# The order of TensorE's products in a two-layer decoder trunk: kinds in larger batches, wide passes grouped by width, low parts last in the head

## The chip, the cores and the metric

The kernel runs on one core of one Trainium2 chip. Its metric is the device time of one execution in microseconds: 427.88 us is the median of three runs before the change (427.61 to 428.37). The profile shows one further execution.

## What is computed

The reference is a trunk of two layers for 256 tokens of width 1024, in float32. Layer 0 makes one input projection of its normalised tokens, and its columns feed three groups of heads: a sparse attention with a compressed, a selected and a window branch (8 heads), a causal block attention (8 heads), and attention to 256 memory tokens (4 heads). Each group is gated, and one output projection adds the result to the tokens. Layer 1 does the same with retention (4 heads of width 256 and values of width 512) and a second memory attention. Cut to its frame:

```python
h = rms_norm(x, norm_g)
(nq, nkc, ..., ng, nz, mq, mk, mv, mz, eq, ez) = _split(h @ w_in, EVEN_SPLITS)
a_out = nsa_attention(rot(nq), kc, vc, rot(nks), heads(nvs), rot(nkw), heads(nvw), gates)
b_out = moba_attention(rot(mq), rot(mk), heads(mv))
m_out = memory_attention(heads(eq), mem_n, w_mem_kv)
x = x + concat([a_out * silu(nz), b_out * silu(mz), m_out * silu(ez)]) @ w_out   # layer 0
...
r_out = head_group_norm(retention(q, k, v))
x = x + concat([r_out * silu(rz), m_out * silu(ez)]) @ w_out                     # layer 1
return rms_norm(x, final_norm_g)
```

## The kernel before

Nearly all of the work is projections, and each of them is done with operands split in two: a high part that is rounded to the type fp32r, and a low part that is the rest. `split` makes the two parts of a loaded block of weights (`raw`): ScalarE writes the high part (`whi`) and VectorE the low part (`wlo`), so the low part is always the later one. A product of full precision is then three products in fp32r: high by high, high by low, and low by high (`mm3`).

TensorE runs four kinds of product here, which the planner numbers: 0 is fp32r on the full array, 1 is float32 on the full array (the 128x128 transposes above all), 2 is float32 with 64 rows of the array (the scores of a pair of heads), and 3 is float32 with 64 columns (the weights by the values). A float32 product that is no transpose runs as two passes and stands as two records in the profile.

The projections come in three shapes. `project` and its sisters have 512 columns of weights as the moving operand, and two banks of PSUM (one for each half of the tokens). `turned_unit` and `first_columns` have the weights as the stationary operand and 256 tokens as the moving one. `project_wide` has the weights as the stationary operand too and moves both parts of the tokens at once (512 columns) past the high part of the weights, and then the high part of the tokens (256 columns) past the low part; its four rounds of 128 rows (`j`) and its two banks (`ct`) make a unit, and two units (`u`) make a pass.

The order of the instructions is not that of the code. Every operation is recorded by `Plan` first, with its dependences, and `arrange` lists them greedily: twelve rounds of `once`, each followed by `dues`, and the round with the earliest end is kept. In `once` each engine takes the next operation by `order`. TensorE's rule has these parts: an operation that became ready less than 250 ns ago (`SLACK`) comes last; in a stretch of kinds 2 and 3 these come first; in kind 0 an operation of another kind goes ahead only if it has been ready for `HOLD` ns; otherwise the order of recording decides. `turn` is the planner's price for a change of kind. The other engines and the DMA queue on SyncE go by `op.due`, the time by which `dues` says that a result is wanted, worked out backwards from the times (`op.goal`) that TensorE's operations had in the round before. What `fixed()` surrounds (the head: the first two projections, up to `first_rows` of the last unit) is kept in the order of the code.

Names in the rows below and in the profile: `bpj` (3 banks), `bs` (2), `btr`, `bt` and `bo` (1 each) are the eight banks of PSUM; `big` holds the split tokens (`xh`, `xl`), `y` and `ym` the split outputs of the heads; `p` and `pt` are the weights of a softmax and their transposes; `vcr` and `yf` are the compressed values and a gated output before its split. All engine instructions are issued from one line, so that they are told apart by these names.

The prediction speaks of the head (`first_rows`, `turned_unit`), of the wide passes (`project_wide`), and of `sparse_pair`, which fills the one bank `bo` and has it emptied by a multiply of `gated` on VectorE (`yf<-bo,v`) before the next pair may begin to fill it.

Of the kernel before, what the change touches and what calls it, by code (L numbers as in the profile page):

```python
# [16 lines left out]
P = 128  # L17
T = 256
# [36 lines left out]
SLACK = 250  # L55
HOLD = 1000
FETCH = 6000
LEAD = 0


class Plan:
# [158 lines left out]
    def turn(self, mode, kind):  # L220
        if mode == kind:
            return 0
        return 95 * (mode > 1 or kind > 1) + (105 if mode > 1 else 6) * (kind == 0)

# [23 lines left out]
    def dues(self, done):  # L248
        at = None
        for op in done:  # L250
            if op.lane == "PE":
                op.goal = op.t if at is None or op.t < 16000 else max(at, 16000)
                at = op.goal + op.spent
        for op in reversed(done):
            due = op.goal if op.lane == "PE" else 1e9
            for other, full in op.next:
                if not full:
                    due = min(due, other.due - other.cost)
                elif other.lane == "PE":
                    due = min(due, other.goal - self.LAG["PE"] - LEAD * (other.kind > 0))  # L260
                else:
                    due = min(due, other.due - other.cost - self.LAG[other.lane] - (FETCH if other.lane == "SP" else self.TAIL[other.lane]))
            op.due = due

    def once(self):
# [8 lines left out]
        while len(done) < len(ops):  # L274
# [30 lines left out]
            for other, full in op.next:  # L305
                other.held -= 1
                if full:
                    other.at = max(other.at, t if other.lane == l == "PE" else op.end + self.LAG[other.lane])
                if not other.held:
                    ready[other.lane].append(other)  # L310
# [22 lines left out]
def trunk(  # L333
# [125 lines left out]
    def turned_unit(ps, lhs, wh, wl, kts, cts):  # L459

        hi, lo = lhs
        for ct in cts:
            for j, kt in enumerate(kts):
                c = slice(j * 512 + ct * P, j * 512 + ct * P + P)
                mm3(ps[ct // 2][:, (ct % 2) * T : (ct % 2 + 1) * T], wh[:, c], wl[:, c], hi[:, kt], lo[:, kt],
                    kt == 0 and ct % 2 == 0, kt == KT - 1, True)

    def project_turned(src, idx, lhs):

        ps = [bank("pj") for _ in range(2)]  # L470
        for kt, wh, wl in units(src, idx, 512):
            turned_unit(ps, lhs, wh, wl, (kt, kt + 1), range(4))
        return ps

# [13 lines left out]
    def project_wide(src, parts, both):  # L488

        for idx, half in parts:  # L490
            ps = [bank("pj") for _ in range(2)]
            for u in range(2):
                raw = load(tl("raw", [P, 1024], NRAW),
                           src[idx + u].rearrange("p (k c) -> p k c", k=4)[:, :, half * 256 : half * 256 + 256])
                wh, wl = split(raw, 1024)
                for ct in range(2):
                    for j in range(4):
                        kt = 4 * u + j
                        c = slice(j * 256 + ct * P, j * 256 + ct * P + P)
                        PE.matmul(ps[ct], wh[:, c], both[:, kt].rearrange("p h t -> p (h t)"), start=kt == 0, stop=False, skip_group_check=True)  # L500
                        PE.matmul(ps[ct][:, T:], wl[:, c], both[:, kt, 0], start=False, stop=kt == KT - 1,
                                  skip_group_check=True)
            e = tl("rot_a", [P, 512], 2).rearrange("p (k t) -> p k t", k=2)
# [100 lines left out]
    def first_rows(wh, wl, kts):  # L604

        for j, kt in enumerate(kts):
            for tok in range(2):
                ts = slice(tok * P, (tok + 1) * P)
                cs = slice(j * 512, (j + 1) * 512)
                mm3(ps_k[tok], xh[:, kt, ts], xl[:, kt, ts], wh[:, cs], wl[:, cs], kt == 0, kt == KT - 1)  # L610

# [737 lines left out]
```

## Time and profile before

| what | value |
|---|---|
| median of the runs shown | 427.88 us |
| time of the profiled execution | 428.38 us |
| span of its trace | 426.6 us |
| last product of TensorE issued | about 420 us into the span |
| TensorE busy | 418.1 us, 2312 records |
| VectorE busy | 325.7 us |
| ScalarE busy | 253.5 us |
| bytes moved | 74.21 MB |

The profiled execution lies 1.8 us over its span and 0.5 us over the median. Its records give a start and a length for each instruction. A length on TensorE includes the time in the pipeline, so lengths of neighbours overlap, and what a product costs is read from the distance between starts. Rows that merge several instructions give the first start; the distance to the next row's start, divided by their count, is the pace.

### The profile page before, as it was taken

The page shows a single profiled execution, that of the slowest core. Times are in us where ns is not written, and L with a number is a line of the kernel's source. Part 1 is how long each engine was busy: PE and PEld are TensorE (multiplying, and loading weights), DVE is VectorE, ACT ScalarE, POOL GpSimd, SP SyncE. Part 2 cuts the span into 40 slices and gives each one's busy share as a digit, 9 for nine tenths or more (in the row PEclk, how much of TensorE's full clock was granted, in tenths as well). Part 3 has the DMA queues.
Part 4 walks back from the last instruction along what each step waited for, and adds up shares of the span by engine and source line. Part 5 has one row for each costly group of instructions (what it writes and reads, how often), then busy time and mean ns, then how long its engine had stood idle before and what let it go on. Part 6 is the DMA issues. An engine that isn't in the chain of part 4 may idle for free.

```text
span 426.6 us, 6506 instructions
## 1 busy us (share of the span) xinstructions
PE 418.1 (98%) x2312; PEld 343.9 (81%) x2312; DVE 325.7 (76%) x744; ACT 253.5 (59%) x477; POOL 3.8 (1%) x11
## 2 busy tenths in 40 slices
PE   8999999999999999999999999999999999999994
PEld 7888988777777787778888888888888888888883
DVE  3789998999897476856978887786997578684624
ACT  4856638997886447945556743754553456653503
POOL 0000000000000000000000000000000000000001
PEclk9999999999999999999999999999999999999999
DMA  7988754331755844452485544365366546457302
GB/s 229 398 297 279 242 195 135 115 101 32 265 192 150 298 127 131 140 164 92 151 251 181 159 141 164 118 205 189 103 219 200 166 141 213 132 169 244 130 2 98
DMA packets 36976, 74.21 MB, mean 174 GB/s; under 512 B 3024, under 2 KB 22736, under 8 KB 36944
## 3 DMA queue, kind: packets, MB, share of 16 engines
q1 hardware_dynamic: 36512, 73.27, 52.2%
q10 hardware_dynamic: 432, 0.52, 0.3%
q8 instruction: 18, 0.29, 0.3%
q14 instruction: 14, 0.11, 0.1%
HBM read 72.74 MB, written 1.05 MB: 173 GB/s over the span
## 4 chain that ended last, share of the span: by engine, by line
PE 92%; DVE 3%; DMA 2%; ACT 1%; issue 0%; DVEq 0%; ACTq 0%
PE bpj L329 70%; PE bs L329 9%; PE btr L329 5%; PE bt L329 4%; PE bo L329 4%; DMA v<-in_xT 2%; DVE wlo L329 1%; DVE tmp L329 1%; DVE v L329 1%; DMA raw<-in_w 1%; ACT whi L329 0%; DVE p L329 0%; ACT big L329 0%; DVE rot_a L329 0%; ACT rot_a L329 0%
## 5 line engine op out<-in xcount | busy, mean ns | idle before, releaser
L329 DVE TENSOR_TENSOR wlo<-raw,whi 128x1024 fp32r<-128x1024 f32 (+3 forms) x127 | 147.0, 1165 | 56.9 <-ACT whi L329 54.4
L329 ACT CAST whi<-raw 128x1024 fp32r<-128x1024 f32 (+3 forms) x127 | 127.3, 1004 | 90.7 <-PE bpj L329 49.4
L329 PE MATMUL bpj<-whi,big 128*128 128x512 f32 (+1 forms) x496 | 150.0, 389 | 0.0
L329 PEld LDWEIGHTS bpj<-whi,big 128*128 128x128 f32 x496 | 91.3, 188 | 18.5 <-issue 1.3
L329 PE MATMUL bpj<-big,whi 128*128 128x512 f32 (+1 forms) x320 | 96.7, 382 | 0.0
L329 PE MATMUL bpj<-wlo,big 128*128 128x512 f32 (+1 forms) x248 | 87.0, 390 | 0.0
L329 PE MATMUL bpj<-big,wlo 128*128 128x256 f32 x288 | 62.7, 284 | 0.2 <-DVE wlo L329 0.2
L329 PEld LDWEIGHTS bpj<-big,wlo 128*128 128x128 f32 x288 | 52.5, 189 | 9.6 <-DVE wlo L329 0.6
L329 PEld LDWEIGHTS bpj<-big,whi 128*128 128x128 f32 x320 | 52.1, 191 | 4.2 <-issue 1.4
L329 PEld LDWEIGHTS bpj<-wlo,big 128*128 128x128 f32 x248 | 46.3, 188 | 9.4 <-issue 1.1
L329 PE MATMUL bpj<-whi,y 128*128 128x512 f32 x84 | 29.2, 396 | 0.0
L329 ACT ACTIVATE p<-p,mx 128x128 f32<-128x128 f32 (+1 forms) x48 | 21.5, 450 | 1.9 <-DVE mx L329 1.9
L329 ACT COPY pt<-bt 128x384 f32<-128x384 f32 (+1 forms) x32 | 16.1, 504 | 10.8 <-PE bt L329 9.4
L329 PEld LDWEIGHTS bpj<-whi,y 128*128 128x128 f32 x84 | 15.8, 188 | 3.1
L329 PE MATMUL bt<-cst,p 128*128 128x128 f32 x104 | 17.2, 278 | 0.0
L329 ACT ACTIVATE v<-bpj,rstd 128x512 f32<-128x512 f32 (+1 forms) x18 | 12.3, 684 | 7.9 <-PE bpj L329 7.9
L329 PE MATMUL bpj<-wlo,y 128*128 128x512 f32 x42 | 16.5, 393 | 0.0
L329 DVE CUSTOM_DVE_ANT_0 p<-bs,cst 128x128 f32<-128x128 f32 (+1 forms) x48 | 14.5, 353 | 2.4 <-PE bs L329 2.4
L329 PEld LDWEIGHTS bt<-cst,p 128*128 128x128 f32 x104 | 12.2, 140 | 4.8 <-issue 1.3
L329 DVE TENSOR_SCALAR p<-p,sm 128x256 f32<-128x256 f32 (+1 forms) x48 | 14.2, 323 | 1.0
L329 DVE TENSOR_TENSOR rot_a<-bpj,rot_a 128x256 f32<-128x256 f32 x32 | 13.3, 419 | 2.0 <-ACT rot_a L329 1.7
L329 ACT COPY rot_a<-bpj 128x256 f32<-128x256 f32 x32 | 11.7, 369 | 3.6 <-PE bpj L329 3.5
(229 smaller groups left out, 503.0 us busy)
## 6 DMA issues: line engine op xcount, KB each, us to landing
raw<-in_w SPq DMA_DIRECT2D x84, 512.0 KB, 4.2
raw<-in_wout SPq DMA_DIRECT2D x28, 512.0 KB, 3.9
raw<-in_w SPq DMA_DIRECT2D x15, 256.0 KB, 6.2
v<-in_xtok SPq DMA_DIRECT2D x4, 512.0 KB, 6.5
raw<-in_w SPq DMA_DIRECT2D x4, 280.0 KB, 3.7
v<-in_w SPq DMA_DIRECT2D x2, 512.0 KB, 4.9
raw<-in_memT SPq DMA_DIRECT2D x2, 512.0 KB, 3.6
raw<-in_memtok SPq DMA_DIRECT2D x2, 512.0 KB, 3.6
```

The lines of the kernel that those rows point to most:

```text
L329: getattr(self.engines[op.lane], method)(*args, **kw)
```

## The change

The change has three parts, and computes the same sums.

The planner. `HOLD` goes from 1000 to 2000; the prices in `turn` go up (from 105 to 150 and from 6 to 50); an operation of another kind has its goal moved back by what slack it has, up to 3000 ns (`RELAX`); and a product that depends on an earlier product counts as ready at once (0.0) and not from the time at which that one was issued. With the last, the products of one bank follow each other as they were recorded, where they took turns with another bank before.

The wide passes. All products with the high part come before those with the low part: over both banks in the first unit, and bank by bank in the second.

The head. `first_rows` and `turned_unit` go over the high weights first, with both parts of the tokens, and use the low weights last. `project_turned`, which nothing calls, is gone.

```diff
--- before.py
+++ after.py
@@ -53,9 +53,10 @@
 ROUNDS = 12
 SLACK = 250
-HOLD = 1000
+HOLD = 2000
 FETCH = 6000
 LEAD = 0
+RELAX = 3000
 
 class Plan:
@@ -220,7 +221,7 @@
     def turn(self, mode, kind):
         if mode == kind:
             return 0
-        return 95 * (mode > 1 or kind > 1) + (105 if mode > 1 else 6) * (kind == 0)
+        return 95 * (mode > 1 or kind > 1) + (150 if mode > 1 else 50) * (kind == 0)
     def arrange(self):
         ops = self.ops
@@ -252,7 +253,7 @@
                 op.goal = op.t if at is None or op.t < 16000 else max(at, 16000)
                 at = op.goal + op.spent
         for op in reversed(done):
-            due = op.goal if op.lane == "PE" else 1e9
+            due = 1e9
             for other, full in op.next:
                 if not full:
                     due = min(due, other.due - other.cost)
@@ -260,6 +261,9 @@
                     due = min(due, other.goal - self.LAG["PE"] - LEAD * (other.kind > 0))
                 else:
                     due = min(due, other.due - other.cost - self.LAG[other.lane] - (FETCH if other.lane == "SP" else self.TAIL[other.lane]))
+            if op.lane == "PE":
+                spare = due - op.spent - self.TAIL["PE"] - op.goal
+                op.goal += min(max(spare, 0), RELAX) if op.kind else 0
             op.due = due
     def once(self):
@@ -305,7 +309,7 @@
             for other, full in op.next:
                 other.held -= 1
                 if full:
-                    other.at = max(other.at, t if other.lane == l == "PE" else op.end + self.LAG[other.lane])
+                    other.at = max(other.at, 0.0 if other.lane == l == "PE" else op.end + self.LAG[other.lane])
                 if not other.held:
                     ready[other.lane].append(other)
         return free["PE"], done
@@ -459,18 +463,11 @@
     def turned_unit(ps, lhs, wh, wl, kts, cts):
         hi, lo = lhs
-        for ct in cts:
-            for j, kt in enumerate(kts):
-                c = slice(j * 512 + ct * P, j * 512 + ct * P + P)
-                mm3(ps[ct // 2][:, (ct % 2) * T : (ct % 2 + 1) * T], wh[:, c], wl[:, c], hi[:, kt], lo[:, kt],
-                    kt == 0 and ct % 2 == 0, kt == KT - 1, True)
-
-    def project_turned(src, idx, lhs):
-
-        ps = [bank("pj") for _ in range(2)]
-        for kt, wh, wl in units(src, idx, 512):
-            turned_unit(ps, lhs, wh, wl, (kt, kt + 1), range(4))
-        return ps
+        for w, x in ((wh, hi), (wh, lo), (wl, hi)):
+            for ct in cts:
+                for j, kt in enumerate(kts):
+                    PE.matmul(ps[ct // 2][:, (ct % 2) * T : (ct % 2 + 1) * T], w[:, j * 512 + ct * P : j * 512 + ct * P + P],
+                              x[:, kt], start=False, stop=kt == KT - 1 and w is wl, skip_group_check=True)
     def project_rows(src, idx, lhs, cols=512):
@@ -493,13 +490,14 @@
                 raw = load(tl("raw", [P, 1024], NRAW),
                            src[idx + u].rearrange("p (k c) -> p k c", k=4)[:, :, half * 256 : half * 256 + 256])
                 wh, wl = split(raw, 1024)
-                for ct in range(2):
-                    for j in range(4):
-                        kt = 4 * u + j
-                        c = slice(j * 256 + ct * P, j * 256 + ct * P + P)
-                        PE.matmul(ps[ct], wh[:, c], both[:, kt].rearrange("p h t -> p (h t)"), start=kt == 0, stop=False, skip_group_check=True)
-                        PE.matmul(ps[ct][:, T:], wl[:, c], both[:, kt, 0], start=False, stop=kt == KT - 1,
-                                  skip_group_check=True)
+                for cts in ((0, 1),) if u == 0 else ((0,), (1,)):
+                    for w in (wh, wl):
+                        for ct in cts:
+                            for j in range(4):
+                                kt = 4 * u + j
+                                out, x = (ps[ct], both[:, kt].rearrange("p h t -> p (h t)")) if w is wh else (ps[ct][:, T:], both[:, kt, 0])
+                                PE.matmul(out, w[:, j * 256 + ct * P : j * 256 + ct * P + P], x, start=kt == 0 and w is wh,
+                                          stop=kt == KT - 1 and w is wl, skip_group_check=True)
             e = tl("rot_a", [P, 512], 2).rearrange("p (k t) -> p k t", k=2)
             for ct in range(2):
                 S.copy(e[:, ct], ps[ct][:, T:])
@@ -603,11 +601,11 @@
     def first_rows(wh, wl, kts):
-        for j, kt in enumerate(kts):
-            for tok in range(2):
-                ts = slice(tok * P, (tok + 1) * P)
-                cs = slice(j * 512, (j + 1) * 512)
-                mm3(ps_k[tok], xh[:, kt, ts], xl[:, kt, ts], wh[:, cs], wl[:, cs], kt == 0, kt == KT - 1)
+        for x, w in ((xh, wh), (xl, wh), (xh, wl)):
+            for j, kt in enumerate(kts):
+                for tok in range(2):
+                    PE.matmul(ps_k[tok], x[:, kt, tok * P : (tok + 1) * P], w[:, j * 512 : (j + 1) * 512],
+                              start=kt == 0 and x is xh and w is wh, stop=kt == KT - 1 and w is wl)
     with plan.fixed():
         for kt in range(2):
```

The order of TensorE's instructions at three places follows. In these rows the engine is TensorE, each row is a product or several alike, out<-in.

The head, at the first projection's third round of rows (`bs_66` and `bs_67` are the two banks of `first_rows`, `bpj_64` and `bpj_65` those of `turned_unit`). Before:

```order
L329 MATMUL bs_66_126<-whi_25_85,big_12_72 128x512
L329 MATMUL bs_66_126<-wlo_29_89,big_12_72 128x512
L329 MATMUL bs_66_126<-whi_25_85,big_12_72 128x512
L329 MATMUL bs_67_127<-whi_25_85,big_12_72 128x512
L329 MATMUL bs_67_127<-wlo_29_89,big_12_72 128x512
L329 MATMUL bs_67_127<-whi_25_85,big_12_72 128x512
L329 MATMUL bpj_64_124<-big_12_72,whi_26_86 128x256 x2
L329 MATMUL bpj_64_124<-big_12_72,wlo_30_90 128x256
L329 MATMUL bpj_64_124<-big_12_72,whi_26_86 128x256 x2
L329 MATMUL bpj_64_124<-big_12_72,wlo_30_90 128x256
L329 MATMUL bpj_65_125<-big_12_72,whi_26_86 128x256 x2
L329 MATMUL bpj_65_125<-big_12_72,wlo_30_90 128x256
```

And now:

```order
L333 MATMUL bs_66_126<-whi_25_85,big_12_72 128x512
L333 MATMUL bs_67_127<-whi_25_85,big_12_72 128x512
L333 MATMUL bs_66_126<-whi_25_85,big_12_72 128x512
L333 MATMUL bs_67_127<-whi_25_85,big_12_72 128x512
L333 MATMUL bs_66_126<-wlo_29_89,big_12_72 128x512
L333 MATMUL bs_67_127<-wlo_29_89,big_12_72 128x512
L333 MATMUL bpj_64_124<-big_12_72,whi_26_86 128x256 x2
L333 MATMUL bpj_65_125<-big_12_72,whi_26_86 128x256 x2
L333 MATMUL bpj_64_124<-big_12_72,whi_26_86 128x256 x2
L333 MATMUL bpj_65_125<-big_12_72,whi_26_86 128x256 x2
L333 MATMUL bpj_64_124<-big_12_72,wlo_30_90 128x256 x2
L333 MATMUL bpj_65_125<-big_12_72,wlo_30_90 128x256 x2
```

In each group of six products the two with `wlo` stood second and fifth and now stand last; in the group of twelve narrow ones they follow each high pair before and now come after all eight.

The wide passes, around the two small products of the compression (`bs_66<-w_0_54,yf_48`): the second unit of one pass (`whi_25`, `wlo_29`) ends and the first unit of the next (`whi_26`, `wlo_30`) begins. Before:

```order
L329 MATMUL bpj_64_124<-big_12_72,whi_25_85 128x512
L329 MATMUL bpj_79_139<-big_12_72,whi_25_85 128x512
L329 MATMUL bs_66_126<-w_0_54_114,yf_48_108 128x64
L329 MATMUL bpj_79_139<-big_12_72,wlo_29_89 128x256
L329 MATMUL bpj_64_124<-big_12_72,wlo_29_89 128x256
L329 MATMUL bpj_65_125<-big_12_72,whi_26_86 128x512
L329 MATMUL bpj_64_124<-big_12_72,whi_25_85 128x512
L329 MATMUL bs_66_126<-w_0_54_114,yf_48_108 128x64
L329 MATMUL bpj_64_124<-big_12_72,wlo_29_89 128x256
L329 MATMUL bpj_64_124<-big_12_72,whi_25_85 128x512
L329 MATMUL bpj_65_125<-big_12_72,wlo_30_90 128x256
L329 MATMUL bpj_64_124<-big_12_72,wlo_29_89 128x256
```

And now:

```order
L333 MATMUL bpj_64_124<-big_12_72,wlo_29_89 128x256 x4
L333 MATMUL bpj_65_125<-big_12_72,whi_26_86 128x512 x4
L333 MATMUL bpj_79_139<-big_12_72,whi_26_86 128x512 x4
L333 MATMUL bpj_65_125<-big_12_72,wlo_30_90 128x256 x4
L333 MATMUL bpj_79_139<-big_12_72,wlo_30_90 128x256 x2
L333 MATMUL bs_66_126<-hid_84_144,w_0_54_114 64x30
L333 MATMUL bs_66_126<-w_0_54_114,yf_48_108 128x64 x2
L333 MATMUL bpj_79_139<-big_12_72,wlo_30_90 128x256 x2
L333 MATMUL bpj_65_125<-big_12_72,whi_27_87 128x512 x4
```

Before, products of 512 and of 256 columns and three banks alternate; now four products of one bank follow each other, and the low parts of the first unit come after the high parts of both banks.

The pairs of heads of the sparse attention, from the values of the first pair (`bo_81<-pt`) on; `rot_a` and `p` are transposed here. Before:

```order
L329 MATMUL bo_81_141<-pt_18_78,s_1_34_94 64x256 x2
L329 MATMUL bo_81_141<-pt_18_78,s_1_34_94 64x128 x2
L329 MATMUL bo_81_141<-pt_17_77,s_1_34_94 64x256 x2
L329 MATMUL bo_81_141<-pt_17_77,s_1_34_94 64x128 x2
L329 MATMUL btr_73_133<-cst_59_119,rot_a_44_104 128x128 x4
L329 MATMUL bpj_65_125<-big_13_73,whi_26_86 128x512
L329 MATMUL bpj_79_139<-big_13_73,whi_26_86 128x512
L329 MATMUL bo_81_141<-s_4_88_148,vcr_0_55_115 128x256
L329 MATMUL bpj_65_125<-big_13_73,wlo_30_90 128x256
L329 MATMUL bpj_79_139<-big_13_73,wlo_30_90 128x256
L329 MATMUL bo_81_141<-s_4_88_148,vcr_0_56_116 128x256
L329 MATMUL bpj_65_125<-big_13_73,whi_26_86 128x512
```

And now:

```order
L333 MATMUL bo_81_141<-pt_18_78,s_1_34_94 64x256 x2
L333 MATMUL bo_81_141<-pt_18_78,s_1_34_94 64x128 x2
L333 MATMUL bo_81_141<-pt_17_77,s_1_34_94 64x256 x2
L333 MATMUL bo_81_141<-pt_17_77,s_1_34_94 64x128 x2
L333 MATMUL bs_66_126<-s_0_33_93,v_5_9_69 128x128
L333 MATMUL bs_67_127<-s_0_33_93,v_5_9_69 128x128
L333 MATMUL bs_66_126<-s_0_33_93,v_5_9_69 128x256
L333 MATMUL bs_67_127<-s_0_33_93,v_5_9_69 128x256
L333 MATMUL btr_73_133<-cst_59_119,rot_a_44_104 128x128 x4
L333 MATMUL bt_68_128<-cst_59_119,p_1_61 128x128 x3
L333 MATMUL bo_81_141<-s_4_88_148,vcr_0_55_115 128x256
L333 MATMUL bo_81_141<-s_4_88_148,vcr_0_56_116 128x256
```

Before, the scores of the next pair had been issued ahead of the values, and after the values and one set of transposes products of `big` go on, with the compressed values (`vcr`) between them. Now the values, the scores of a later pair, two sets of transposes and the compressed values of the next pair stand in one block.

Counted over the whole program, a record of one kind is followed by one of another 191 times before and 145 times now:

| from | to | before | now |
|---|---|---|---|
| fp32r | 64 rows or columns | 24 | 16 |
| full float32 array | 64 rows or columns | 5 | 8 |
| 64 rows or columns | fp32r | 16 | 13 |
| 64 rows or columns | full float32 array | 13 | 11 |
| 64 columns | 64 rows | 2 | 5 |
| fp32r | full float32 array | 61 | 44 |
| full float32 array | fp32r | 70 | 48 |

Two neighbouring fp32r products differ in width 301 times before and 112 times now.

## The prediction

> **What bounds the kernel now.** I read the busy times first, then the chain that ended last, then stretches, then the order of time.
>
> ```profile
> PE 418.1 (98%) x2312; PEld 343.9 (81%) x2312; DVE 325.7 (76%) x744; ACT 253.5 (59%) x477; POOL 3.8 (1%) x11
> PE 92%; DVE 3%; DMA 2%; ACT 1%; issue 0%; DVEq 0%; ACTq 0%
> ...
> 14.00:50.00 36.00, 36.00 (x222) 32.34 (x221) 32.07 (x69) 25.57 (x39) 0.00 (x0) 1.00 0.86 298
> 50.00:115.00 65.00, 64.60 (x459) 51.52 (x458) 58.92 (x200) 48.98 (x132) 0.84 (x2) 1.00 0.46 150
> 115.00:200.00 85.00, 85.00 (x471) 64.99 (x470) 59.57 (x136) 54.12 (x124) 0.00 (x0) 1.00 0.50 162
> ```
>
> TensorE (PE) is busy for 98% of the span and holds 92% of the chain. In the stretches (length, then busy time of PE, PEld, DVE, ACT, POOL) it is full from 14 us on, at a granted clock of 1.00. So the time is the sum of the distances between the starts of its records, and a change of order is worth what it takes from these. VectorE (DVE) comes next: 58.92 of 65 us in the stretch from 50 to 115. It can take a gain back there.
>
> **What a product costs, and a change of width.** These pieces of the chain (start, length, engine and bank, count) are runs of one width; the rows of time after them alternate two of 256 with two of 512 columns.
>
> ```profile
> 19.03 2.87 PE bpj L329 x24
> 409.54 5.67 PE bpj L329 x25
> ...
> 228.06 0.40 PE L329 MATMUL bpj<-big,wlo 128*128 128x256 f32 x2
> 228.29 0.63 PE L329 MATMUL bpj<-big,whi 128*128 128x512 f32 x2
> ...
> 231.55 0.39 PE L329 MATMUL bpj<-big,wlo 128*128 128x256 f32 x2
> ```
>
> Narrow: 2.87 / 24 = 0.1196 us. Wide: 5.67 / 25 = 0.2268 us. From 228.06 to 231.55 stand 10 narrow and 10 wide products, which at these paces take 3.464 us; they took 3.49, so ten changes of width cost 0.026, or 2.6 ns each (rounding of the starts allows 1 to 4). The change has 189 fewer (301 to 112): 0.49 us by that, 0 if it is rounding alone. I take -0.4.
>
> [...]
>
> **Changes of kind.** The rows show two stops of scores (64 rows of the array) between fp32r products, the second with transposes behind it, and one stop of transposes alone.
>
> ```profile
> 225.75 0.40 PE L329 MATMUL bpj<-big,wlo 128*128 128x256 f32 x2
> 226.08 1.14 PE L329 MATMUL bs<-s,s 64*128 64x256 f32 x8
> 227.14 0.51 PE L329 MATMUL bpj<-big,whi 128*128 128x512 f32 x1
> 227.48 0.28 PE L329 MATMUL bpj<-big,wlo 128*128 128x256 f32 x1
> ...
> 233.86 0.66 PE L329 MATMUL bt<-cst,p 128*128 128x128 f32 x4
> 234.27 0.48 PE L329 MATMUL bpj<-big,whi 128*128 128x512 f32 x1
> 234.59 0.40 PE L329 MATMUL bpj<-big,wlo 128*128 128x256 f32 x2
> ...
> 101.77 0.49 PE L329 MATMUL bt<-cst,p 128*128 128x128 f32 x3
> 102.10 0.60 PE L329 MATMUL btr<-cst,rot_a 128*128 128x128 f32 x4
> 102.45 0.48 PE L329 MATMUL bpj<-big,wlo 128*128 128x256 f32 x2
> 102.77 0.85 PE L329 MATMUL bpj<-big,whi 128*128 128x512 f32 x3
> ...
> 103.69 0.49 PE L329 MATMUL bt<-cst,p 128*128 128x128 f32 x3
> 104.12 0.93 PE L329 MATMUL bs<-s,v 64*128 64x128 f32 x8
> ```
>
> Into the scores from fp32r: two narrow products take 225.75 to 226.08, 0.33 where 0.24 is their pace: 0.09. Out: eight passes of 256 columns take 1.06, where eight narrow products take 0.96: 0.10; and the first wide product after them 0.34 (227.14 to 227.48) for 0.23: 0.11. So back to fp32r costs 0.21. To transposes: four of them and the wide product behind take 233.86 to 234.59, 0.73, where the stop of seven gives 0.109 each: 101.77 to 102.45 is 0.68, and the two narrow ones behind 0.32 for 0.24, so 0.76 / 7. Four are 0.44, with the wide one 0.67, so 0.06 more and with the 0.10 before it 0.16. From transposes into scores: 103.69 to 104.12 is 0.43 for three, 0.33 by that pace: 0.10. Between columns and rows I take the 0.10 of leaving.
>
> By the counts of the order: 8 entries fewer from fp32r (-0.72), 3 more from the full array (+0.30), 3 fewer returns to fp32r (-0.63), 2 fewer to the full array (-0.32), 3 more from columns to rows (+0.30). **Kinds: -1.07**, and between -0.7 and -1.3 if each price is off by a rounding of the starts. A stop of transposes costs no more than its transposes, by the seven (0.109 each with the return, 0.33 / 3 = 0.11 inside); of 17 entries and 22 returns less I take 0.1 us, between 0 and 0.2. The raised prices in the planner (150 and 50) are no cost of the chip; they act through these counts alone.
>
> **The head.** Here TensorE waits. The rows are the two last stalls for a low weight and what sets their ends.
>
> ```profile
> 10.10 0.62 ACT L329 CAST whi<-raw 128x512 fp32r<-128x512 f32 x1 [1.87 <-DMA raw<-in_w]
> 10.77 0.49 PE L329 MATMUL bs<-whi,big 128*128 128x512 f32 x1
> 11.50 0.50 PE L329 MATMUL bs<-wlo,big 128*128 128x512 f32 x1 [0.23 <-DVE wlo L329]
> 11.83 0.63 PE L329 MATMUL bs<-whi,big 128*128 128x512 f32 x2
> 11.98 2.50 ACT L329 CAST whi<-raw 128x512 fp32r<-128x512 f32 x4
> 12.62 2.60 DVE L329 TENSOR_TENSOR wlo<-raw,whi 128x512 fp32r<-128x512 f32 x4
> 12.76 0.41 PE L329 MATMUL bpj<-big,whi 128*128 128x256 f32 x2
> 13.36 0.39 PE L329 MATMUL bpj<-big,wlo 128*128 128x256 f32 x1 [0.20 <-DVE wlo L329]
> 14.66 0.40 PE L329 MATMUL bs<-whi,big 128*128 128x512 f32 x1
> ```
>
> Six products start at 10.77, when ScalarE has cast weights that landed at 10.10; no order of products moves that, so whatever an earlier group gains is lost here. Now the group runs through: one product with a restart (0.33, as from 11.50 to 11.83) and five of 0.23 end at 12.25. The twelve narrow products behind need the first of the four casts (11.98 + 0.62 = 12.60) and start at about 12.65, where they started at 12.76. Their low weight is there at 12.62 + 0.65 = 13.27, four products before it is wanted (12.65 + 0.10 + 8 x 0.12 = 13.71), so that they end at 12.65 + 0.10 + 1.44 = 14.19 and not at 14.66. **Head: -0.46.** Next late is that cast, and behind it ScalarE's others at 0.62 each, faster than six wide products (1.4). TensorE is full from 14 to 50, so the gain lasts unless VectorE gives it back. Bounds: 0 and -0.6.
>
> **Waits elsewhere.** The rows show the largest, and what empties the one bank `bo`.
>
> ```profile
> 56.60 0.30 PE L329 MATMUL bs<-tmp,v 128*64 128x30 f32 x2
> 57.24 2.05 PE L329 MATMUL bs<-tmp,v 128*64 128x30 f32 x62 [0.34 <-DVE tmp L329]
> ...
> 112.72 0.92 PE L329 MATMUL bpj<-big,whi 128*128 128x512 f32 x2
> 113.48 0.40 PE L329 MATMUL bpj<-big,wlo 128*128 128x256 f32 x2
> ...
> 98.42 1.52 PE L329 MATMUL bo<-pt,s 128*64 128x256 f32 x16
> 99.87 0.66 PE L329 MATMUL btr<-cst,rot_a 128*128 128x128 f32 x4
> 99.99 0.42 DVE L329 TENSOR_TENSOR yf<-bo,v 128x256 f32<-128x256 f32 x1
> ...
> 188.79 1.23 DVE L329 TENSOR_TENSOR wlo<-raw,whi 128x1024 fp32r<-128x1024 f32 x1 [2.53 <-ACT whi L329]
> ```
>
> Two records at 56.60 take 0.64 and should take 0.1: 0.5 of waiting for the compression's sums on VectorE. Two wide products at 112.72 take 0.76 for 0.45: 0.3, in the wide passes, whose banks are taken turn by turn. Bank by bank, the first of a pass is full four wide and four narrow products (1.4 us) ahead of the second, so the second wait has cover; the first has about as much as before (16 wide and 14 narrow products stand between the last transposes and these sums). On the other side stands `bo`: it is free 0.54 us after the values end (99.87 to 99.99 + 0.42), and the next pair's compressed values now come after scores (0.85) and three or seven transposes (0.33 or 0.76), 1.2 to 1.6 us, enough if VectorE is free, but 0.55 short of it where a `wlo` of 1.23 stands ahead of the multiply (1.23 + 0.42 + 0.1 - 1.2). Bounds -0.8 and +1.65 (three refills in the sparse pairs). I take -0.4, half of what may go, since both chains of the wide passes get earlier.
>
> **Sum:** -0.4 - 1.07 - 0.1 - 0.46 - 0.4 = -2.43. The profiled execution took 428.38 (span 426.6 and 1.8 around it), 0.5 over the median of 427.88; it would take 425.95, and the median **425.4**. Its own range is 424.4 to 426.6. PSUM traffic, bytes and the work of the other engines stay the same.
>
> **The rivals.**
>
> More: the waits of 0.8 go altogether, the kinds give 1.3, the widths 0.75 (4 ns each), transposes 0.2, the head 0.6: -3.65, 424.2. For it: TensorE alone bounds most stretches. Against: it takes every bound at once. 0.10.
>
> The refills of `bo` stall three times: +1.65 and nothing gained from waits (+0.4): -0.38, 427.5. For it: 91% of VectorE from 50 to 115. Against: with 1.2 us of cover for 0.54, some 0.6 us of other work may stand ahead of the multiply at no cost. 0.12.
>
> The change doesn't do what it says: the cost that I read at edges belongs to the products themselves, and only the head gains: 427.4. For it: single edges are read to 0.01 us from sums of a few records. Against: the first wide product after a stop took 0.34 and 0.32 us in two places, for a pace of 0.23. 0.06.
>
> Slower: the same bank on all eight pairs and two pairs of memory heads, ten refills with a `wlo` ahead, 10 x 0.55 = 5.5, against the gain without waits (-2.03): +3.5, 431.4. It decides from a stop on in which fewer than 1.75 us of products stand between the values and the next use of `bo`. For it: `HOLD` lets other kinds wait 1 us longer and then brings them at once. Against: VectorE has 25 of 85 us free from 115 to 200. 0.07.
>
> **How the numbers follow.** The forecast has 0.65. About 0.2% (0.86 us) is what a measurement here can tell from no change, so faster means below 427.0. Faster: 0.65 + 0.10 and half of the mildest refill case, 0.81 in all; same 0.12; slower 0.07. The range of 8 in 10 leaves out the slower rival and part of the edges: 424.1 to 427.4.
>
> **What would show it.** In the profile after: no TensorE wait for `wlo` in the head and the first `bs<-whi` behind the twelve narrow products near 14.2; 24 stops of scores or values for 29, and at each first wide product after one still 0.34 us; alternating widths gone from the passes; `bo<-s,vcr` without idle time ahead. I am wrong if TensorE's records show idle time for `bo` or `wlo` between 50 and 135 us of more than 1.5 us, or if edges are fewer and the distances within blocks grow.

## The result, and the profile after

The changed kernel took **425.22 us** (median of six runs, 425.02 to 425.31), where the kernel before took 427.76 (six runs beside them, 427.33 to 428.37): a ratio of 0.9938, with a 95% interval of 0.9926 to 0.9951. The gain is 2.54 us. The profiled execution took 425.25, with a span of 423.5.

The page of the changed kernel: busy times and the chain that ended last. Behind it two of the stretches that were shown of before (length, then busy time of PE, PEld, DVE, ACT and POOL, granted clock, DMA share, GB/s).

```profile
PE 415.7 (98%) x2312; PEld 343.4 (81%) x2312; DVE 325.9 (77%) x744; ACT 253.2 (60%) x477; POOL 3.8 (1%) x11
PE 92%; DMA 5%; DVE 1%; ACT 1%; issue 0%; DVEq 0%; ACTq 0%
...
14.00:50.00 36.00, 35.78 (x214) 31.31 (x213) 31.08 (x69) 24.78 (x37) 0.00 (x0) 1.00 0.89 301
50.00:115.00 65.00, 65.00 (x471) 53.28 (x470) 62.22 (x197) 50.17 (x129) 0.83 (x2) 1.00 0.57 182
```

TensorE still sets the time: full from 50 to 115 us, with the same number of records and 2.4 us less of busy time. VectorE has 62.22 of 65 us from 50 to 115, where it had 58.92, and TensorE doesn't wait for it there. The waits of TensorE, before (L329) and now (L333), each with its total, count and longest:

```profile
PE bs L329 <- DVE wlo L329: 0.5, 2, 0.2
PE bs L329 <- DVE tmp L329: 0.3, 1, 0.3
...
PE bpj L329 <- DVE wlo L329: 0.2, 1, 0.2
```

```profile
PE bt L333 <- POOL kcbd L333: 1.0, 1, 1.0
PE bs L333 <- ACT whi L333: 0.3, 1, 0.3
```

The three waits for `wlo` are gone, and so is that for `tmp` at 57.24. The head of the changed kernel in order of time, TensorE and ScalarE's casts:

```profile
10.34 1.09 PE L333 MATMUL bs<-whi,big 128*128 128x512 f32 x4
11.27 0.62 PE L333 MATMUL bs<-wlo,big 128*128 128x512 f32 x2
11.72 1.12 PE L333 MATMUL bpj<-big,whi 128*128 128x256 f32 x8
12.68 0.64 PE L333 MATMUL bpj<-big,wlo 128*128 128x256 f32 x4
13.16 1.09 PE L333 MATMUL bs<-whi,big 128*128 128x512 f32 x4
...
10.58 2.53 ACT L333 CAST whi<-raw 128x512 fp32r<-128x512 f32 x4
```

The group of six and the group of twelve run through. The first `bs<-whi` behind them starts at 13.16 instead of 14.66, but that is not all the order's work: the four casts began at 10.58 where they began at 11.98, because the weights and tokens had landed earlier in this execution. Over the fourteen profiles on record, with the old head or the new, they began anywhere from 10.36 to 11.98.

For a view of the whole I split the time of TensorE in two (worked out from all records of the traces): *steps*, the sum over all products of the median distance that a product of its kind, between those two neighbours, has in the traces; and *waits*, what single distances are longer than that by more than 30 ns. Before: steps 414.2, waits 4.9. Now: steps 412.6, waits 2.9. So these two executions differ by 1.6 us of steps and 1.9 of waits. The two add to 3.5, while the last product is issued 3.1 earlier (416.99 for 420.12 us into the span), since distances shorter than the median aren't counted: each half is good to some tenths. The profiled execution before was itself 0.6 over its median, with its late casts.

### The profile page after: what moved, and what is told of

Its sections match the earlier page's. It is cut to its first block, busy times and chain, and to the rows that moved or that the text cites. A ratio compares the mean times of both kernels' runs of the same rounds, so it can differ in the third digit from the quotient of the medians.

```text
span 423.5 us, 6508 instructions
## 1 busy us (share of the span) xinstructions
PE 415.7 (98%) x2312; PEld 343.4 (81%) x2312; DVE 325.9 (77%) x744; ACT 253.2 (60%) x477; POOL 3.8 (1%) x11
## 4 chain that ended last, share of the span: by engine, by line
PE 92%; DMA 5%; DVE 1%; ACT 1%; issue 0%; DVEq 0%; ACTq 0%
PE bpj L333 71%; PE bs L333 8%; PE btr L333 5%; PE bo L333 4%; PE bt L333 4%; DMA raw<-in_w 3%; DMA v<-in_xT 1%; DVE v L333 1%; DVE p L333 0%; ACT rot_a L333 0%; ACT whi L333 0%; ACT big L333 0%; ACT ss L333 0%; DVE wlo L333 0%; DVE ss L333 0%
## 5 line engine op out<-in xcount | busy, mean ns | idle before, releaser
L333 DVE TENSOR_TENSOR wlo<-raw,whi 128x1024 fp32r<-128x1024 f32 (+3 forms) x127 | 146.8, 1165 | 49.8 <-ACT whi L333 49.0
L333 ACT CAST whi<-raw 128x1024 fp32r<-128x1024 f32 (+3 forms) x127 | 127.1, 1004 | 81.7 <-PE bpj L333 48.1
L333 PE MATMUL bpj<-whi,big 128*128 128x512 f32 (+1 forms) x496 | 156.6, 388 | 0.0
L333 PEld LDWEIGHTS bpj<-whi,big 128*128 128x128 f32 x496 | 91.6, 188 | 18.7 <-issue 1.3
L333 PE MATMUL bpj<-wlo,big 128*128 128x512 f32 (+1 forms) x248 | 95.8, 386 | 0.0
L333 PE MATMUL bpj<-big,whi 128*128 128x512 f32 (+1 forms) x320 | 79.5, 376 | 0.2
L333 PEld LDWEIGHTS bpj<-big,whi 128*128 128x128 f32 x320 | 53.1, 190 | 8.3 <-issue 0.9
L333 PEld LDWEIGHTS bpj<-wlo,big 128*128 128x128 f32 x248 | 46.6, 188 | 9.1 <-issue 0.7
L333 PEld LDWEIGHTS bpj<-big,wlo 128*128 128x128 f32 x288 | 41.7, 190 | 4.5 <-issue 0.7
L333 PE MATMUL bpj<-big,wlo 128*128 128x256 f32 x288 | 45.2, 284 | 0.0
L333 PE MATMUL bpj<-whi,y 128*128 128x512 f32 x84 | 28.1, 393 | 0.0
L333 ACT COPY pt<-bt 128x384 f32<-128x384 f32 (+1 forms) x32 | 16.1, 504 | 16.4 <-PE bt L333 16.3
L333 ACT ACTIVATE p<-p,mx 128x128 f32<-128x128 f32 (+1 forms) x48 | 21.4, 448 | 1.8 <-DVE mx L333 1.8
L333 PEld LDWEIGHTS bpj<-whi,y 128*128 128x128 f32 x84 | 15.6, 188 | 3.7 <-issue 0.5
L333 ACT COPY rot_a<-bpj 128x256 f32<-128x256 f32 x32 | 11.8, 367 | 10.3 <-PE bpj L333 9.9
L333 PE MATMUL bt<-cst,p 128*128 128x128 f32 x104 | 17.1, 277 | 0.0
L333 PE MATMUL bpj<-wlo,y 128*128 128x512 f32 x42 | 16.4, 391 | 0.0
L333 PEld LDWEIGHTS bt<-cst,p 128*128 128x128 f32 x104 | 12.4, 140 | 4.8 <-issue 2.6
L333 DVE CUSTOM_DVE_ANT_0 p<-bs,cst 128x128 f32<-128x128 f32 (+1 forms) x48 | 14.7, 352 | 1.1 <-PE bs L333 1.1
L333 DVE TENSOR_SCALAR p<-p,sm 128x256 f32<-128x256 f32 (+1 forms) x48 | 14.4, 324 | 1.3
L333 DVE TENSOR_TENSOR rot_a<-bpj,rot_a 128x256 f32<-128x256 f32 x32 | 13.4, 420 | 1.4 <-ACT rot_a L333 1.1
L333 ACT ACTIVATE v<-bpj,rstd 128x512 f32<-128x512 f32 (+1 forms) x18 | 12.4, 687 | 2.9 <-PE bpj L333 2.8
```

The lines of the kernel that those rows point to most:

```text
L333: getattr(self.engines[op.lane], method)(*args, **kw)
```

## The experiments

Two sorts of variant are needed. In the first, one part of the change is undone and the planner arranges anew. In the second the order of all engines is kept by a table of numbers, from the one kernel or the other, and only the products inside the edited place stand otherwise; that leaves the planner out. All compute the same sums. Each was compared with the kernel before on its own chip (427.69 to 427.86 us there).

| variant | changes of kind | of width | steps | waits | time, us | ratio, 95% |
|---|---|---|---|---|---|---|
| before | 191 | 301 | 414.2 | 4.9 | 427.76 | |
| changed | 145 | 112 | 412.6 | 2.9 | 425.22 | 0.9926–0.9951 |
| 1 head alone | 184 | 322 | 413.9 | 10.4 | 435.45 | 1.0156–1.0206 |
| 2 old head | 142 | 112 | 412.6 | 5.6 | 427.14 | 0.9968–0.9992 |
| 3 old wide passes | 143 | 510 | 413.0 | 4.7 | 427.01 | 0.9971–0.9988 |
| 4 no staying in a kind | 170 | 114 | 413.8 | 6.0 | 428.53 | 1.0013–1.0031 |
| 5 order kept, old head | 145 | 112 | 412.6 | 3.2 | 425.53 | 0.9937–0.9963 |
| 6 order of before kept, new head | 191 | 301 | 414.2 | 4.0 | 427.54 | 0.9988–1.0006 |
| 7 order kept, old wide passes | 145 | 510 | 413.2 | 4.2 | 426.45 | 0.9960–0.9980 |
| 8 order kept, scores cut | 193 | 111 | 420.3 | 5.0 | 435.21 | 1.0159–1.0188 |
| 9 order kept, transposes cut | 255 | 109 | 413.0 | 4.1 | 426.18 | 0.9955–0.9975 |
| 10 `HOLD` 4000 | 122 | 115 | 412.4 | 18.2 | 440.87 | 1.0270–1.0337 |
| 11 only the rule of 0.0 | 157 | 112 | 413.1 | 10.6 | 432.66 | 1.0076–1.0134 |
| 12 old planner | 182 | 343 | 413.8 | 9.1 | 433.31 | 1.0104–1.0164 |

### One part alone, or undone, with the planner free

**1, the head alone.** The kernel before, with `first_rows` and `turned_unit` of the change.

```diff
-                mm3(ps_k[tok], xh[:, kt, ts], xl[:, kt, ts], wh[:, cs], wl[:, cs], kt == 0, kt == KT - 1)
+        for x, w in ((xh, wh), (xl, wh), (xh, wl)):
...
```

> The kernel before with the new order in the head alone (low weights last in first_rows and turned_unit). Its order has 184 changes of kind for 191 and 322 changes of width for 301, so almost only the head differs. By the prediction's terms: head -0.46, the rest 0.0 to -0.05, 427.3 us beside 427.76 before. The rival is that the head gains as much as the changed kernel's profile shows at the first narrow-and-wide rounds (the group of six at 14.66 us before starts at 13.16 now), -1.5: 426.3 us. A third way is that VectorE takes it back by 60 us: 427.7 us.

It took 435.45, 7.7 us more than before, where 0.46 less had been expected. Steps are no worse (413.9), but waits went from 4.9 to 10.4; most of what was added lies between 28 and 35 us, far behind the edit. The planner has only reordered; what it did there is seen best in variant 11.

**2, the old head** in the changed kernel, and **3, the old order inside the wide passes**.

> The changed kernel with the old order in the head (low weights in between). Changes of kind 142 for 145, of width 112 for 112. By the prediction's head term +0.46: 425.7 us beside 425.22 of the changed kernel. By the rival (1.5 us, as the profile shows): 426.7 us. If VectorE takes the head's gain back: 425.2 us.

> The changed kernel with the old order inside the wide passes (high and low product alternate). Changes of kind 143 for 145, of width 510 for 112, so 398 changes of width are added and little else. By the prediction's 2.1 ns each (0.4 us for 189): +0.84, 426.1 us. If a change of width costs nothing: 425.2 us. At the upper bound of 4 ns: 426.8 us.

427.14 and 427.01: each lost most of the gain. Neither part is worth 1.8 or 1.9 us by itself, as variants 5 and 7 show; steps are within 0.4 of the changed kernel, and the waits are others (5.6 and 4.7 for 2.9).

**4, without the rule that stays in a kind** of products.

```diff
-            if mode > 1:
-                return (2 - (op.kind > 0) - (op.kind > 1), 0, op.rank)
-            if mode == 1:
-                return (0 if op.kind else 1, 0, op.rank)
```

> The changed kernel without the planner's rule that keeps TensorE in a kind once it is in it. Changes of width 114 for 112, of kind 170 for 145 (fp32r to 64 rows or columns 25 for 16, back 17 for 13, full array to them 4 for 8 and back 12 for 11, columns and rows 1 for 5). By the prediction's prices these are +1.0 us: 426.2 us. By the rival that the edges cost nothing beyond their products: 425.2 us. Above 427 would speak for waits that come with it, which the profile would show.

428.53, above the kernel before. Steps rose by 1.2 for 25 more changes of kind, waits by 3.1. One of them is the refill of `bo` that was feared:

```profile
96.58 1.52 PE L329 MATMUL bo<-pt,s 128*64 128x256 f32 x16
98.03 0.55 PE L329 MATMUL bt<-cst,p 128*128 128x128 f32 x3
98.42 0.60 PE L329 MATMUL btr<-cst,rot_a 128*128 128x128 f32 x4
98.77 0.48 PE L329 MATMUL bpj<-big,whi 128*128 128x512 f32 x1
99.96 0.50 PE L329 MATMUL bo<-s,vcr 128*128 128x256 f32 x2 [0.71 <-DVE yf L329]
```

So the rival's mechanism exists: the compressed values could have started 1.2 us behind the last of the values (98.03) and stand for another 0.7 until VectorE has emptied the bank. It is not a `wlo` that holds VectorE up, as the prediction had it, but rotations and four sums for a softmax, without a gap until the multiply begins at 99.48. In the changed kernel, in the same part, scores and two sets of transposes lie between, 1.6 us, and there is no idle time:

```profile
95.33 1.52 PE L333 MATMUL bo<-pt,s 128*64 128x256 f32 x16
96.78 0.93 PE L333 MATMUL bs<-s,v 64*128 64x128 f32 x8
97.64 0.66 PE L333 MATMUL btr<-cst,rot_a 128*128 128x128 f32 x4
98.13 0.49 PE L333 MATMUL bt<-cst,p 128*128 128x128 f32 x3
98.38 0.48 PE L333 MATMUL bo<-s,vcr 128*128 128x256 f32 x2
```

### The order kept by a table

The planner's `arrange` is replaced; the edit under test is the one named.

```diff
-    def arrange(self):
+    def arrange(self):
+        raw = zlib.decompress(base64.b85decode(ORDER))
+        line = [self.ops[i] for i in struct.unpack(f"<{len(raw) // 2}H", raw)]
...
```

**5, the old head under the order of the change**, and **6, the new head under the order of before** (the edit of variant 1, back and forth).

> The order of every engine is the changed kernel's, kept by a table of numbers instead of the planner; only the products of the head stand in their old order. All changes of kind and width as in the changed kernel (145 and 112). By the prediction's head term: +0.46, 425.7 us. If the head is worth the 1.5 us between the two profiles (14.66 and 13.16): 426.7 us. If the 1.9 us that the old head cost with the planner free to reorder belong to the head itself: 427.1 us.

> The order of every engine is the kernel before's, kept by a table of numbers; only the products of the head stand in the new order. By the head term: -0.46, 427.3 us beside 427.76. If the head of itself makes the 435.45 us that it made with the planner free to reorder: 435 us; if the planner's other choices made those, 427.3.

5 took 425.53, 0.3 above the changed kernel (0.5 by the ratios, whose intervals overlap); 6 took 427.54, 0.3 below the kernel before (0.1 by the ratio, whose interval holds 1). So the times alone don't show the head's gain. The traces are sharper. In variant 5 the stall for `wlo` stands in the group of twelve again:

```profile
11.88 0.47 PE L405 MATMUL bpj<-big,whi 128*128 128x256 f32 x2
12.57 0.39 PE L405 MATMUL bpj<-big,wlo 128*128 128x256 f32 x1 [0.23 <-DVE wlo L405]
...
13.87 0.40 PE L405 MATMUL bs<-whi,big 128*128 128x512 f32 x1
...
11.19 1.87 ACT L405 CAST whi<-raw 128x512 fp32r<-128x512 f32 x3
```

With the new head and casts at 11.05 (variant 1) the same product stands at 13.24:

```profile
13.24 1.09 PE L329 MATMUL bs<-whi,big 128*128 128x512 f32 x4
...
11.05 1.86 ACT L329 CAST whi<-raw 128x512 fp32r<-128x512 f32 x3
```

From the cast to it: 2.68 us with the old head, 2.19 with the new, 0.49 less. That is the head's worth at like landing. It repeats: all three profiles with the old head (before, 2 and 5) have 2.68, and all six with the new head whose casts began at 11.05 or later have 2.18 to 2.20. With earlier casts, as in the changed kernel's own profile (10.58 to 13.16, 2.58), TensorE still has the products of the group before to do, and the distance is no measure of the head.

**7, the old order inside the wide passes, everything else kept.**

```diff
-                for cts in ((0, 1),) if u == 0 else ((0,), (1,)):
-                    for w in (wh, wl):
...
+                for ct in range(2):
+                    for j in range(4):
...
```

> The order of every engine is the changed kernel's, kept by a table; only inside each unit of the wide passes the products stand as before, high and low alternating. Changes of width 510 for 112, all changes of kind the same. By the prediction's 2.1 ns each: +0.84, 426.05 us. If a change of width costs nothing: 425.2. If the 1.8 us of the run with the planner free belong to the widths (4.5 ns each): 427.0.

426.45, 1.2 above the changed kernel (1.4 by the ratios), with 398 more changes of width. But it isn't the widths. Here they alternate, with one narrow and one wide product for each 0.35 us:

```profile
235.51 0.40 PE L405 MATMUL bpj<-big,whi 128*128 128x512 f32 x1
...
238.64 0.60 PE L405 MATMUL bt<-cst,p 128*128 128x128 f32 x4
```

Nine pairs take 238.64 − 235.51 = 3.13 us; at the paces of the prediction, 9 x 0.3464 = 3.118. Three stretches of the two traces that hold the same products and no wait differ by +0.08 us for 54 more changes, −0.09 for 102 and +0.005 for 18: nothing. By the steps of the whole it is 0.55 / 398 = 1.4 ns. The rest of the 1.2 is waits:

```profile
PE bpj L405 <- ACT whi L405: 0.6, 1, 0.6
PE bs L405 <- DVE sc L405: 0.4, 1, 0.4
PE bo L405 <- DVE yf L405: 0.2, 1, 0.2
```

The first of them stands in the head, at 8.87, where TensorE waits for ScalarE's cast; the others wait for VectorE, in an order that was planned for other products. That they come from banks filled a little later is likely, and not shown.

**8, 24 stops of scores or values cut in two by one fp32r product**, and **9, 55 stops of transposes cut in the same way.**

```diff
+            half = len(op.calls) // 2
+            op.calls, rest.calls = op.calls[:half], op.calls[half:]
...
+            out += [line[n], rest]
```

> The order of every engine is the changed kernel's, kept by a table; each of 24 stops of scores or values is cut in two by the next fp32r product that depends on nothing between. 24 entries (0.09) and 24 returns (0.21) more, nothing else: by the prediction's prices +7.2, 432.4 us. If the edges cost nothing beyond their products: 425.2. If the price is half of what I read from the rows: 428.8.

> The changed kernel's order kept by a table; 55 stops of transposes are cut in two by the next fp32r product (0>1 entries 44 to 99, returns 48 to 103; scores, values and weights as they were). By the prediction a stop of transposes costs nothing beside its transposes, at most 0.2 us for 17 entries: 425.2 to 425.9 us. If they paid like the stops of scores and values (0.42 each): 425.2 + 23 = 448. If only an entry and a return as after four transposes at 233.86 (0.06 to 0.16 each): 428.5 to 434.

8 took 10.0 us more than the changed kernel, 0.42 for each cut, where 0.30 had been expected. Uncut (changed kernel) and cut, the same scores:

```profile
222.72 0.28 PE L333 MATMUL bpj<-big,wlo 128*128 128x256 f32 x1
222.94 1.13 PE L333 MATMUL bs<-s,s 64*128 64x256 f32 x8
224.00 0.62 PE L333 MATMUL bpj<-big,wlo 128*128 128x256 f32 x3
```

```profile
230.97 0.70 PE L439 MATMUL bs<-s,s 64*128 64x256 f32 x4
231.60 0.39 PE L439 MATMUL bpj<-big,wlo 128*128 128x256 f32 x1
231.92 0.70 PE L439 MATMUL bs<-s,s 64*128 64x256 f32 x4
232.55 0.50 PE L439 MATMUL bpj<-big,wlo 128*128 128x256 f32 x2
```

Eight passes take 224.00 − 222.94 = 1.06 us, four take 231.60 − 230.97 = 0.63. So a pass costs (1.06 − 0.63) / 4 = 0.1075, and a stop 0.63 − 4 x 0.1075 = 0.20 inside itself, besides the 0.09 before and 0.11 behind it: 0.40. The records of single passes show where the 0.20 lies: the first two passes of the stop take 0.32 and the last two 0.31, two between them 0.216. Compared cut by cut, with the same products on both sides and no new wait, scores (64 rows) pay 0.39 to 0.41 us and values (64 columns) 0.33 to 0.36. The column of steps has only 7.7 of the 10.0, because a median by neighbours doesn't tell the first pair of a stop from the others; the rest of that cost stands there as waits. The records show that this time is added at the edges of a stop; what TensorE does in it they don't show.

9 took 426.18, 1.0 above the changed kernel (1.15 by the ratios), of which 0.4 is steps: 0.007 us for each of the 55 cuts. Most of the rest is two waits, of 0.6 us at 200.65 and of 0.8 at 281.75. A stop of transposes is next to no stop. They are float32 as well, so a change of type alone doesn't make the price in variant 8. That the part of the array makes it would fit, but scores and transposes differ in more (two passes against one), and no run here separates the two.

### The planner's numbers

**10, `HOLD` 4000 for 2000; 11, the planner of before with only the rule that a product behind a product is ready at once; 12, the planner of before whole, with the new head and wide passes.**

```diff
-HOLD = 2000
+HOLD = 4000
```

```diff
-HOLD = 2000
+HOLD = 1000
-RELAX = 3000
...
-        return 95 * (mode > 1 or kind > 1) + (150 if mode > 1 else 50) * (kind == 0)
+        return 95 * (mode > 1 or kind > 1) + (105 if mode > 1 else 6) * (kind == 0)
...
-            due = 1e9
+            due = op.goal if op.lane == "PE" else 1e9
```

> The changed kernel with HOLD 4000 for 2000: 23 stops of scores or values for 24, 32 entries of transposes for 44, 122 changes of kind for 145. If the counts decide: 0.42 less for the stop and 0.2 by the other kinds' prices, 424.6 to 424.9 us. If the waits decide (each other order of the planner brings its own): 425.5 to 428.

> The changed kernel with the planner of before (HOLD 1000, prices 105 and 6, goals not moved back), but products behind products ready at once (0.0): 26 stops for 24, 157 changes of kind for 145, 112 changes of width as in the changed kernel. By the counts: two stops at 0.42, 426.1 us. If the waits decide: anything from 425 to 430.

> The planner of before whole, with the new head and the new order of the wide passes: 29 stops, 182 changes of kind, 343 of width. By the counts: five stops at 0.42 and the widths at 0 to 1.5 ns, 427.3 to 427.7 us, the head 0.3 to 0.5 below that: 427.0. If the waits decide, as with the new head alone: 428 to 436.

Counts would have put them at 424.7, 426.1 and 427; they took 440.87, 432.66 and 433.31, all slower than before. Steps do what the counts say (412.4, 413.1, 413.8); the waits don't follow from them. In 10 the largest single wait comes from SyncE's queue, with the start and length of each group of its transfers:

```profile
115.69 0.90 SPq L333 DMA_DIRECT2D v<-in_xtok  x2
162.50 0.33 SPq L333 DMA_DIRECT2D v<-in_grow  x1
162.93 9.01 SPq L333 DMA_DIRECT2D raw<-in_wout  x7
```

```profile
SPq L333 <- DVE sm L333: 51.1, 2, 45.9
```

```profile
166.65 0.66 PE L333 MATMUL bt<-cst,p 128*128 128x128 f32 x4
170.37 0.96 PE L333 MATMUL bpj<-whi,y 128*128 128x512 f32 x3 [3.07 <-ACT whi L333]
```

The load of `in_grow` waits 45.9 us for VectorE's sums of a softmax, and the weights of the output projection are queued behind it; TensorE has batched its scores, has no projection left among them from 161.93 on, and stands 3.07 us for the weights. That is a fifth of the 15.3 us of waits that this order adds. Six more waits, 3.6 us together, are of transposes for ScalarE to empty their bank; the rest is spread.

In 11 (and 12, and 1) the place is the end of the head. VectorE's rows and TensorE's, of variant 11:

```profile
27.94 1.23 DVE L329 TENSOR_TENSOR wlo<-raw,whi 128x1024 fp32r<-128x1024 f32 x1
...
32.80 3.49 DVE L329 TENSOR_TENSOR wlo<-raw,whi 128x1024 fp32r<-128x1024 f32 x3
```

```profile
29.22 1.19 PE L329 MATMUL bs<-wlo,big 128*128 128x512 f32 x4 [0.46 <-DVE wlo L329]
30.68 0.51 PE L329 MATMUL bpj<-whi,big 128*128 128x512 f32 x1 [0.27 <-DVE tmp L329]
31.81 0.44 PE L329 MATMUL btr<-cst,rot_a 128*128 128x128 f32 x2 [0.62 <-DVE rot_a L329]
32.93 0.52 PE L329 MATMUL btr<-cst,rot_a 128*128 128x128 f32 x2 [0.69 <-DVE rot_a L329]
34.07 0.80 PE L329 MATMUL bpj<-wlo,big 128*128 128x512 f32 x1 [0.62 <-DVE wlo L329]
```

VectorE makes the tables of the rotation and the rotated rows in one piece, and one `wlo` between 27 and 32.8 us; in the changed kernel three stand among them (27.08, 28.36 and 31.07), and TensorE doesn't wait. The three variants have in common the new head and the old way of setting due times; with the order of before kept (variant 6) the new head does no harm. Which part of the change's planner makes VectorE put `wlo` among the tables stays open.

## Why the prediction was right, and where its steps were not

The total was right: 425.4 forecast, 425.22 measured, −2.43 against −2.54 us. What bounds the kernel was right too: TensorE's records and the distances between them. That the total came so near is in part luck, since the terms were off both ways:

**Widths (−0.4) were too large.** Measured 0 to 1.4 ns a change, so 0 to −0.26 for 189. The 2.6 ns came from ten changes and a difference of 0.026 us, which is the rounding of two starts; the forecast named that bound and took the other end. The 0 that it gave for rounding alone was nearer than what was taken.

**Kinds (−1.07) were too small**, and the step that failed is the price of leaving, 0.10. It was taken as what eight passes cost over eight narrow products of 0.1196; a pass of the scores costs 0.1075, so a stop has 0.20 inside. The prices that were read at single rows came back: the first wide product behind a stop takes 0.34 us in the changed kernel as before. With 0.20 for 0.10 in each price that holds it (3 returns at 0.31, 2 to the full array at 0.26, 3 from columns to rows at 0.10 to 0.20, if columns pay as rows do; cut by cut a stop of columns was some 0.05 cheaper), the sum is −0.72 + 0.30 − 0.93 − 0.52 + 0.30 to 0.60, −1.27 to −1.57, an estimate from these prices and the counts of the order.

**Transposes (−0.1) were right**: 0.007 us for each stop, −0.12 to −0.15 for 17 entries and 22 returns.

Together these three make −1.4 to −2.0 by the corrected prices; the steps of the traces give −1.6, the forecast had −1.57. Two errors of opposite sign made the sum good, which is luck.

**The head (−0.46) was right**: 0.49 at like landing. The times of variants 5 and 6 (0.1 to 0.5) agree without being clear of noise. The start at 14.2 was not met (13.16), since the casts began 1.4 us earlier in the profiled execution; measured from the cast it was forecast 2.2 us behind it (11.98 to 14.19), and six profiles have 2.18 to 2.20.

**Waits elsewhere (−0.4)**: the two named, and a third at 111.63, are gone, 0.9 us. But the changed kernel has three that weren't there, at 23.27, 48.63 and 280.75, 0.7 together. About −0.2 is left by the profiles, one execution of each kernel. The cost on the other side, refills of `bo`, did not come.

**The rivals.** The refills of `bo`, three or ten of them, are refuted for this order by the rows at 98.38, though variant 4 shows that the mechanism is real at 0.7 us, with other work of VectorE ahead of the multiply than was thought. That edges cost nothing is refuted by variant 8, and that the widths give 0.75 by variant 7.

What the working didn't see is how near another result lay: the seven variants that the planner arranged anew took 427.0 to 440.9, and none of the twelve is faster than the changed kernel (variant 5 lies within the noise of it).

## What to carry to other kernels

Price a stop by its whole round trip, by comparing a long stop with a cut one: here 0.40 us for scores on 64 rows and 0.33 to 0.36 for values on 64 columns, next to nothing for transposes or for the width of the moving operand. Count steps and waits apart: steps follow the counts to a few tenths, waits belong to the one order that the planner has found, and an edit worth half a microsecond (variant 1) cost 7.7 us through them. So judge an edit with the order held fixed, and judge a planner's constant only by the run it gives; where that run is slow, read the waits of the queue of loads and of the engine that makes the low parts.

## What was not expected of the hardware

**The clock fell without a long gap.** In variant 11 the longest single wait of TensorE between 28 and 34 us is 0.7 us, yet the granted clock went to 0.50 there (the column after POOL) and came back only at 40:

```profile
31.00:33.00 2.00, 0.69 (x4) 0.27 (x4) 1.93 (x6) 1.97 (x4) 0.00 (x0) 1.00 0.17 64
33.00:33.50 0.50, 0.45 (x2) 0.13 (x2) 0.50 (x1) 0.50 (x3) 0.00 (x0) 0.66 0.00 0
...
35.00:39.00 4.00, 4.00 (x11) 3.05 (x10) 3.42 (x7) 0.26 (x1) 0.00 (x0) 0.50 0.89 239
...
40.00:40.50 0.50, 0.50 (x3) 0.42 (x3) 0.50 (x2) 0.00 (x0) 0.00 (x0) 1.00 1.03 386
```

By the share in the second row it fell at 33.16 (0.34 of that half microsecond at 0.50), and it lasted 6.8 us. The wide products then stand 0.43 us apart instead of 0.23: twelve of them and parts of two more, 2.7 us on top of the idle time. Variants 1 and 12 had nearly the same idle time (3.4 to 3.6 us busy of six) and no fall of the clock in their profiled executions; over the runs of variants 1, 10, 11 and 12 the mean clock goes from 0.986 to 0.998 and the times are spread by 3 to 5 us, the longer ones mostly at the lower clock (variant 11: 430.66 at 0.996, 433.3 at 0.989). Before the fall stand four waits, of 0.3 to 0.7 us, and from 30.68 us on TensorE had only one fp32r product and four transposes. One longer wait brought no fall in variant 10: TensorE stands 3.07 us ahead of 170.37, and the granted clock of that profiled execution is 1.00 from 165 to 170 us and from 170 to 175. Whether the pauses or the few products between them made the clock fall in variant 11, and why it stayed at 1.00 in variants 1 and 12, no run here shows.

**Passes on half of the array go two by two.** A pass of the scores costs 0.1075 us by the cut and the uncut stop above, less than a narrow fp32r product of the same 256 columns (0.1196). But the records show no single pass of that length: two passes start 6 to 8 ns apart, and the next two 0.216 us after the first. The same holds for the values on 64 columns (0.216 us for two passes of 256 columns). Two float32 passes on the full array don't start together: in the stretch at 66.22 us of the kernel before, the second of 30 columns comes 27 ns behind the first and the next product 0.11 us later.
